# Moving loads to GpSimd's queue, listing first weight chunks one stage earlier, and reordering the end of the last block

## The chip, the cores and the metric

The kernel runs on one core of one Trainium2 chip. The metric is the device time of one execution in microseconds (us). An execution's time is a little longer than its span, which runs from the first to the last instruction of the program.

## What is computed

One residual block on 512 tokens of width 2048, in f32. A normalised input goes through one wide projection; its columns feed three branches and their gates. Each branch has its own output projection, the three are merged by sigmoid gates, and one last projection is added to the residual stream.

```python
h = rms_norm(x, norm_g)
proj = h @ w_in
(c_gate, b_gate, u, conv_z, c_q, c_kv, k_rope_raw, mla_z,
 mem_q, mem_z, g_conv, g_mla, g_mem) = jnp.split(proj, split_at, axis=-1)
conv_y = b_gate * causal_depthwise_conv(c_gate * u, conv_w)
o_conv = (conv_y * jax.nn.silu(conv_z)) @ w_conv_out
mla_y = mla_attention(c_q, c_kv, k_rope_raw, cos, sin, ...)        # 16 heads, chunk mask
o_mla = (mla_y * jax.nn.silu(mla_z)) @ w_mla_out
mem_y = memory_attention(mem_q, mem, ...)                          # 256 tokens, 4 heads
o_mem = (mem_y * jax.nn.silu(mem_z)) @ w_mem_out
merged = sigmoid(g_conv)*o_conv + sigmoid(g_mla)*o_mla + sigmoid(g_mem)*o_mem
x = x + merged @ w_o
```

## The kernel before

TensorE works in a reduced-precision f32 form, so every product is three matmuls: weights and activations are split into a high and a low part (`mm3`, lines 158 to 163). ScalarE rounds a weight chunk to its high part (`whi`), VectorE subtracts it from the raw chunk (`wlo`). The first two matmuls of a panel product need `whi` alone, the third needs `wlo`.

The stages follow each other: key/value projection of the memory tokens (line 510), the wide input projection `w_h` in 64 blocks (line 778), attention with the convolution branch's output projection mixed in (lines 1044 to 1088), memory attention (line 1153), the rest of the convolution's projection (line 1176), the attention's output projection `w_mla_out` in 8 blocks (line 1207), the memory branch's output projection (line 1244), and the last projection `w_o` in 8 blocks (line 1246). Stages named with "blocks" use `panels`: a block is 256 output features, four weight chunks of 512 KB, and per chunk 14 products of 256 columns, which is 42 matmuls. Each raw chunk also needs three sums on VectorE (`pair_weights`, lines 263 to 265) before it is split (268, 269). The first two blocks run their chunks in the order 0,1,2 / 0,1,2 / 3,3, so the last two of the eight activation pairs `xp` are wanted only with the seventh chunk.

Weight chunks are jobs in one Python list, `queue`. `take(ahead)` starts the jobs of the next chunks (load and sums) and converts those up to `ahead` in front. Jobs listed after a stage can't be started in it. The raw tile has three buffers, `whi` and `wlo` two each.

The order on SyncE (SP, the engine that issues the loads) and on TensorE is the order of the Python program; both queues are in order. The order on VectorE, ScalarE and GpSimd comes from a planner that simulates the program; on the chip these queues are in order too.

`gate_blocks` (line 1008) loads the sigmoid gates of the convolution branch; from group 1 on its tile `sb` has two buffers. `mem_pair` (line 1224) merges two output blocks of the memory branch: it loads gate and running sum into one tile `mg` with one buffer (1225, 1226), multiplies and adds (1228, 1229), builds the pair's sums and splits them (ScalarE line 249, VectorE line 250) into the activations of `w_o`. `make_mla` (1194) loads a gate block in each block of `w_mla_out`, and in block 6 six tiles of the memory branch. `finish` (735) stores sigmoid gates through ScalarE's queue (774). `panel_steps` (274) runs a block and adds its four PSUM banks up afterwards (301 to 307); `finish_o` (1271) adds the residual and stores.

## Time and profile before

| | us |
|---|---|
| three runs | 2202.24, 2200.24, 2202.16 (median 2202.16) |
| the profiled execution | 2199.24 |
| its span | 2197.4 |
| TensorE busy | 2132.2 (97%) |
| VectorE busy | 1744.8 (79%) |
| ScalarE busy | 1004.2 (46%) |
| GpSimd busy | 110.8 (5%) |
| mean granted TensorE clock | 0.989 |

Busy time of TensorE hides slow stretches: a matmul at a lower granted clock is busy for longer. So the stretches are read by how many matmuls start in them, beside a stretch without any wait.

### The profile page before, as it was taken

What the parts mean: (1) busy time and instruction counts of PE and PEld (TensorE: products, weight loads), DVE (VectorE), ACT (ScalarE), POOL (GpSimd) and SP (SyncE); (2) the same over time, 40 slices, a digit from 0 to 9 for tenths busy, and PEclk for the clock granted to TensorE, in tenths of its full rate; (3) what the DMA queues carried; (4) which work ended last, traced back from release to release, by engine and by line L of the source; (5) the groups of instructions that cost most, each with busy time, mean ns of one, the idle gap of its engine ahead of it and who ended that gap; (6) DMA issues with size and microseconds to landing.
All of it is one profiled execution on the core that took longest, in us unless ns stands there. A gap on an engine that the chain in (4) does not pass through costs nothing.

```text
span 2197.4 us, 38848 instructions
## 1 busy us (share of the span) xinstructions
PE 2132.2 (97%) x16040; PEld 2043.9 (93%) x16040; DVE 1744.8 (79%) x2763; ACT 1004.2 (46%) x1219; POOL 110.8 (5%) x149
## 2 busy tenths in 40 slices
PE   9999999999999999999999999999999899996998
PEld 8789999999999999999999998888888699985998
DVE  6986888888888888889777875888877778657887
ACT  6743444444334444444444444877764433322332
POOL 0000000000000000000000001221211100000000
PEclk9999999999999999999999999999999999998999
DMA  8633433334334334343444446123266855644443
GB/s 328 237 101 135 154 135 126 128 128 134 120 125 135 116 125 136 126 138 133 132 132 147 133 133 225 68 87 113 92 238 226 330 146 168 199 163 172 150 158 116
DMA packets 92289, 334.31 MB, mean 152 GB/s; under 512 B 10768, under 2 KB 11024, under 8 KB 90064
## 3 DMA queue, kind: packets, MB, share of 16 engines
q1 hardware_dynamic: 75024, 268.05, 36.0%
q0 software_dynamic: 8160, 38.54, 5.1%
q10 hardware_dynamic: 8928, 25.25, 3.3%
q8 instruction: 125, 2.05, 0.4%
q14 instruction: 52, 0.43, 0.1%
HBM read 273.34 MB, written 58.46 MB: 151 GB/s over the span
## 4 chain that ended last, share of the span: by engine, by line
PE 84%; DVE 7%; DMA 5%; ACT 3%; issue 1%; POOL 0%; SPq 0%; DVEq 0%; POOLq 0%; ACTq 0%
PE acc L161 15%; PE acc L163 15%; PE acc L162 15%; PE aux L161 12%; PE aux L163 12%; PE aux L162 12%; DVE wlo L269 2%; DMA sb<-gdram 1%; DMA raw<-in_w_h 1%; PE aux L970 1%; DMA amdram<-my 1%; DVE raw L263 1%; PE aux L953 1%; DMA raw<-in_w_mla_out 0%; PE aux L954 0%
## 5 line engine op out<-in xcount | busy, mean ns | idle before, releaser
L268 ACT ACTIVATE whi<-raw 128x1792 fp32r<-128x1792 f32 x304 | 517.4, 1703 | 796.3 <-PE acc L162 363.1
L269 DVE TENSOR_TENSOR wlo<-raw,whi 128x1792 fp32r<-128x1792 f32 x304 | 614.6, 2022 | 205.4 <-ACT whi L268 205.0
L163 PE MATMUL aux<-xp,wlo 128*128 128x256 f32 (+1 forms) x1712 | 479.8, 280 | 4.8 <-DVE wlo L269 4.7
L161 PE MATMUL aux<-xp,whi 128*128 128x256 f32 (+1 forms) x1712 | 480.7, 281 | 0.1
L162 PE MATMUL aux<-xp,whi 128*128 128x256 f32 (+1 forms) x1712 | 479.4, 280 | 0.0
L163 PE MATMUL acc<-xp,wlo 128*128 128x256 f32 x1680 | 469.5, 279 | 3.4 <-DVE wlo L269 3.4
L161 PE MATMUL acc<-xp,whi 128*128 128x256 f32 x1680 | 470.1, 280 | 0.0
L162 PE MATMUL acc<-xp,whi 128*128 128x256 f32 x1680 | 469.1, 279 | 0.0
L163 PEld LDWEIGHTS aux<-xp,wlo 128*128 128x128 f32 (+1 forms) x1712 | 321.3, 188 | 5.7 <-DVE wlo L269 5.7
L161 PEld LDWEIGHTS aux<-xp,whi 128*128 128x128 f32 (+1 forms) x1712 | 321.1, 188 | 0.5 <-ACT whi L268 0.5
L162 PEld LDWEIGHTS aux<-xp,whi 128*128 128x128 f32 (+1 forms) x1712 | 320.4, 187 | 0.0
L163 PEld LDWEIGHTS acc<-xp,wlo 128*128 128x128 f32 x1680 | 315.4, 188 | 4.4 <-DVE wlo L269 4.4
L161 PEld LDWEIGHTS acc<-xp,whi 128*128 128x128 f32 x1680 | 315.3, 188 | 0.0
L162 PEld LDWEIGHTS acc<-xp,whi 128*128 128x128 f32 x1680 | 314.7, 187 | 0.0
L263 DVE TENSOR_TENSOR raw<-raw 128x512 f32<-128x512 f32 x304 | 208.4, 686 | 46.9 <-DMA raw<-in_w_h 32.4
L155 DVE TENSOR_TENSOR wlo<-raw,whi 128x1024 fp32r<-128x1024 f32 (+2 forms) x91 | 101.7, 1121 | 49.9 <-ACT whi L154 49.4
L154 ACT ACTIVATE whi<-raw 128x1024 fp32r<-128x1024 f32 (+2 forms) x91 | 89.0, 978 | 105.5 <-PE acc L162 37.2
L265 DVE TENSOR_TENSOR raw<-raw 128x256 f32<-128x256 f32 x304 | 128.3, 422 | 6.3
L264 DVE TENSOR_TENSOR raw<-raw 128x256 f32<-128x256 f32 x304 | 128.1, 422 | 5.8
L161 PE MATMUL acc<-whi,blk 128*128 128x384 f32 (+1 forms) x224 | 86.1, 384 | 3.6 <-ACT whi L154 3.6
L336 POOL TENSOR_TENSOR rs_r<-rs_t,mhalf 128x2 f32<-128x2 f32 (+2 forms) x71 | 69.4, 987 | 289.9 <-DVE rs_t L335 225.6
L162 PE MATMUL acc<-wlo,blk 128*128 128x384 f32 (+1 forms) x224 | 81.6, 364 | 0.3 <-DVE wlo L155 0.3
(348 smaller groups left out, 3892.8 us busy)
## 6 DMA issues: line engine op xcount, KB each, us to landing
raw<-in_w_h SPq DMA_DIRECT2D x240, 512.0 KB, 3.5
raw<-in_w_mla_out SPq DMA_DIRECT2D x32, 512.0 KB, 3.7
raw<-in_w_o SPq DMA_DIRECT2D x32, 512.0 KB, 3.7
raw<-in_w_mem_kv SPq DMA_DIRECT2D x31, 512.0 KB, 7.3
gdram<-e ACTq DMA_DIRECT2D x24, 512.0 KB, 2.8
raw<-in_w_ukv SPq DMA_DIRECT2D x16, 512.0 KB, 5.5
raw<-in_w_conv_out SPq DMA_DIRECT2D x16, 512.0 KB, 8.9
aadram<-z POOLq DMA_DIRECT2D x8, 896.0 KB, 4.0
```

What stands on the lines that cost most here:

```text
L154: act.activation(hi[:, cols], raw[:, cols], AF.Copy)
L155: vec.tensor_tensor(out=lo[:, cols], in0=raw[:, cols], in1=r32(hi[:, cols]), op=ALU.subtract)
L161: nc.tensor.matmul(o, lhsT=s[0], rhs=m[0], start=start, stop=False, skip_group_check=shared)
L162: nc.tensor.matmul(o, lhsT=s[0], rhs=m[1], start=False, stop=False, skip_group_check=shared)
L163: nc.tensor.matmul(o, lhsT=s[1], rhs=m[0], start=False, stop=stop, skip_group_check=shared)
L263: vec.tensor_tensor(out=f[:, 4:6], in0=f[:, 1:3], in1=f[:, 0:1].to_broadcast([P, 2, 256]), op=ALU.add)
L264: vec.tensor_tensor(out=f[:, 6], in0=f[:, 5], in1=f[:, 1], op=ALU.add)
L265: vec.tensor_tensor(out=f[:, 7], in0=f[:, 6], in1=f[:, 3], op=ALU.add)
L268: act.activation(hi, f[:, 1:8], AF.Copy)
L269: vec.tensor_tensor(out=lo, in0=f[:, 1:8], in1=r32(hi), op=ALU.subtract)
L336: pool.tensor_tensor(out=r, in0=t, in1=mhalf[:, :n], op=ALU.pow)
L953: nc.tensor.matmul(sb[:, :n], lhsT=qr[:, cols], rhs=krh[:, :n], start=False, stop=False)
```

## The change

- The panel work of `w_h` is listed ahead of the memory projection's loop, and that of `w_mla_out` and the memory output's chunks ahead of the last loop over the convolution's projection. The look-ahead of the memory projection becomes a function of the step (2 in steps 8 to 29, else 1).
- Gate loads of convolution groups 1 to 3, and gate and sum loads of `mem_pair`, go from SP's queue to GpSimd's. The last six gate stores go from ScalarE's queue to GpSimd's.
- The six memory tiles are loaded one in each of the blocks 1 to 6 of `w_mla_out`.
- The order of the memory attention's steps among the convolution's is changed (`ORDER_MEM`; a digit is a step of that head, "4w" four units of three matmuls of the convolution).
- In the last chunk of the last block of `w_o` the products are sorted, so that the four PSUM banks finish one after the other; `tail_o` adds them up and the residual, and stores the two halves on ScalarE's and SP's queues.

```diff
-ORDER_MEM = "0 0 1 1 5w 0 0 2 3w 1 1 3 3w 0 0 2 2 3w 1 1 3 3 3w 2 2 2w 3 3 w 2 2 3 3"
+ORDER_MEM = "0 0 4w 1 1 4w 0 0 2 2w 1 1 3 3w 0 0 2 2 w 1 1 3 3 2w 2 2 3w 3 3 w 2 2 3 3"
...
-            whi, wlo = take(ahead)
+            whi, wlo = take(ahead(c) if callable(ahead) else ahead)
...
-            for kk in range(2):
+            each = [(kk, pr) for kk in range(2) for pr in PRODUCTS]
+            if tail is not None and c == nch - 1:
+                each.sort(key=lambda e: PRODUCTS.index(e[1]))
+            for kk, (w, xi, bk, half) in each:
...
         vec.tensor_tensor(out=e[:, 1:6:4], in0=b[0], in1=e[:, 4:5].to_broadcast([P, 2, H]), op=ALU.add)
+        if tail is not None:
+            tail(b, e)
+            yield
+            return
...
+    work = panels(xp, a["w_h"], len(SEQUENCE), lambda n: make(n), lambda n, e: finish(n, e), "aux")
+    queue.insert(32 + 15, [lambda: rotary_weights(), None])
     parts_of_x = all_parts()
...
-                             ahead=2 if grp else 1):
+                             ahead=lambda c: 2 if 0 < 8 * grp + c - 7 < 23 else 1):
...
-            act.dma_start(gdram[GATES[kind, i]], two(e))
+            (act if n < 58 else nc.gpsimd).dma_start(gdram[GATES[kind, i]], two(e))
...
-    work = panels(xp, a["w_h"], len(SEQUENCE), make, finish, "aux")
-    queue.insert(next(at for at in range(len(queue)) if at == 15), [rotary_weights, None])
...
+                nc.sync.dma_start(t, gdram[n])
             else:
                 t = pg.tile([P, 2, S], F32, tag="sb", name="sb", bufs=2)
-            nc.sync.dma_start(t, gdram[n])
+                nc.gpsimd.dma_start(t, gdram[n])
...
     pairs = new_pairs()
+    work = panels(xp, a["w_mla_out"], 8, lambda n: make_mla(n), lambda n, e: finish_mla(n, e))
+    for grp in range(3):
+        upcoming(*plain_jobs([a["w_mem_out"][grp][c] for c in range(4)], 512))
+    for grp in range(2):
+        upcoming(*plain_jobs([a["w_mem_out2"][grp][c] for c in range(4)], 256))
     for n, _ in enumerate(conv):
...
-            if n == 6:
-                for k in range(6):
-                    memory_block(k, pam)
+            if n > 0 and n < 7:
+                memory_block(n - 1, pam)
...
-        nc.sync.dma_start(two(t, 4), gdram[16 + n])
-        nc.sync.dma_start(two(t), mgdram[n])
+        nc.gpsimd.dma_start(two(t, 4), gdram[16 + n])
+        nc.gpsimd.dma_start(two(t), mgdram[n])
...
+    def tail_o(b, e):
+
+        xr = xrs[7]
+        x4 = xr.rearrange("p f (h n) -> p (f h) n", h=2)
+        vec.tensor_tensor(out=x4[:, 1], in0=e[:, 1], in1=x4[:, 1], op=ALU.add)
+        vec.tensor_tensor(out=e[:, 6:8], in0=b[1], in1=e[:, 5:6].to_broadcast([P, 2, H]), op=ALU.add)
+        vec.tensor_tensor(out=x4[:, 0], in0=x4[:, 0], in1=e[:, 7], op=ALU.add)
+        vec.tensor_tensor(out=x4[:, 2:4], in0=x4[:, 2:4], in1=e[:, 6:7].to_broadcast([P, 2, H]), op=ALU.subtract)
+        vec.tensor_tensor(out=x4[:, 0], in0=b[2][:, 0], in1=x4[:, 0], op=ALU.add)
+        nc.scalar.dma_start(out[14 * P:15 * P], xr[:, 0])
+        vec.tensor_tensor(out=x4[:, 2], in0=x4[:, 2], in1=b[1][:, 1], op=ALU.subtract)
+        vec.tensor_tensor(out=x4[:, 3], in0=b[2][:, 1], in1=x4[:, 3], op=ALU.add)
+        nc.sync.dma_start(out[15 * P:16 * P], xr[:, 1])
```

## Rows read from the trace of the kernel before

**Rows 1.** The page, the span in 40 slices: busy tenths of TensorE.
```profile
PE   9999999999999999999999999999999899996998
```
**Rows 2.** Busy time by stretch: length, each engine busy (instructions), granted clock, DMA share, GB/s.
```profile
400.00:420.00 20.00, 20.00 (x172) 20.00 (x172) 17.79 (x25) 7.42 (x6) 0.00 (x0) 1.00 0.36 111
...
107.00:157.00 50.00, 43.07 (x337) 41.43 (x336) 43.02 (x52) 21.45 (x18) 0.10 (x1) 0.97 0.34 110
...
1746.00:1760.00 14.00, 5.15 (x24) 4.75 (x24) 12.16 (x16) 3.29 (x2) 2.16 (x4) 0.63 0.66 237
1900.00:1908.00 8.00, 3.53 (x19) 3.04 (x18) 7.21 (x10) 3.28 (x2) 0.00 (x0) 0.69 0.52 89
2010.00:2042.00 32.00, 13.06 (x89) 12.11 (x87) 24.07 (x34) 10.31 (x7) 0.00 (x0) 0.73 0.46 164
```
**Rows 3.** Waits of TensorE: who waited for whom, us in total, times, longest.
```profile
PE acc L161 <- ACT whi L268: 23.5, 2, 16.0
...
PE aux L343 <- DVE p L1130: 3.0, 1, 3.0
```
**Rows 4.** Timeline of ScalarE, start of w_h: start, us, instruction, idle before and releaser.
```profile
111.49 1.70 ACT L268 ACTIVATE whi<-raw 128x1792 fp32r<-128x1792 f32 x1 [2.81 <-DVE raw L265]
```
**Rows 5.** The page, costliest groups: count, busy us, mean ns of one, idle before.
```profile
L263 DVE TENSOR_TENSOR raw<-raw 128x512 f32<-128x512 f32 x304 | 208.4, 686 | 46.9 <-DMA raw<-in_w_h 32.4
...
L264 DVE TENSOR_TENSOR raw<-raw 128x256 f32<-128x256 f32 x304 | 128.1, 422 | 5.8
```
**Rows 6.** The page, DMA issues: queue, count, KB each, median us to landing.
```profile
gdram<-e ACTq DMA_DIRECT2D x24, 512.0 KB, 2.8
...
acdram<-e POOLq DMA_DIRECT2D x8, 512.0 KB, 3.5
...
mq<-mqdram POOLq DMA_DIRECT2D x4, 1024.0 KB, 10.6
...
mg<-gdram SPq DMA_DIRECT2D x8, 512.0 KB, 3.4
```
**Rows 7.** Timeline of SP's queue at the start of attention.
```profile
1343.36 0.32 SPq L914 DMA_DIRECT2D krl<-krdram  x1
```
**Rows 8.** Timeline of GpSimd: issue of a load.
```profile
1631.82 0.54 POOL L1075 DMA_DIRECT2D mq<-mqdram  x1 [2.40 <-PE aux L343]
```
**Rows 9.** Timeline of VectorE in the memory attention.
```profile
1663.21 1.28 DVE L1118 TENSOR_REDUCE mx<-aux 128x2 f32<-128x512 f32 x2
```
**Rows 10.** Timeline of SP's queue at the start of w_mla_out.
```profile
1738.86 4.06 SPq L1018 DMA_DIRECT2D sb<-gdram  x2
1743.03 1.32 SPq L262 DMA_DIRECT2D raw<-in_w_mla_out  x3
```
**Rows 11.** Timeline of SP's queue in block 6 of w_mla_out.
```profile
1881.33 2.89 SPq L1187 DMA_DIRECT2D am<-amdram  x6
```
**Rows 12.** Timeline of SP's queue at the start of w_o.
```profile
2014.29 0.32 SPq L1225 DMA_DIRECT2D mg<-gdram  x1
...
2015.13 1.40 SPq L262 DMA_DIRECT2D raw<-in_w_o  x3
```
**Rows 13.** Timeline of ScalarE: splits of the first two chunks of w_o.
```profile
2024.92 3.27 ACT L268 ACTIVATE whi<-raw 128x1792 fp32r<-128x1792 f32 x2
```
**Rows 14.** Timeline of VectorE: first product of pairs 0 and 7, split of pair 7.
```profile
1942.06 1.37 DVE L1228 TENSOR_TENSOR mg<-acc,mg 128x512 f32<-128x512 f32 x2 [1.31 <-PE acc L163]
...
2031.29 1.28 DVE L1228 TENSOR_TENSOR mg<-aux,mg 128x512 f32<-128x512 f32 x2
...
2042.11 2.02 DVE L250 TENSOR_TENSOR xo<-mg,xo 128x1792 fp32r<-128x1792 f32 x1
```
**Rows 15.** Timeline of TensorE: the seventh chunk of w_o.
```profile
2061.91 0.28 PE L161 MATMUL acc<-xo,whi 128*128 128x256 f32 x1
```
**Rows 16.** Timeline of VectorE at the end.
```profile
2191.31 0.69 DVE L303 TENSOR_TENSOR e<-aux,e 128x512 f32<-128x512 f32 x1
...
2193.04 1.28 DVE L1274 TENSOR_TENSOR xr<-e,xr 128x512 f32<-128x512 f32 x2
```

More of the change, by code (lines that the diff above doesn't have):

```diff
@@ L272, in body, with panel_steps @@
     later, between = [], []
-    def panel_steps(xp, e, tag, middle=None):
+    def panel_steps(xp, e, tag, middle=None, tail=None):
         d = bank(tag)
@@ L290, in panel_steps @@
                 first, last = c == 0 and kk == 0, c == nch - 1 and kk == 1
-                for w, xi, bk, half in PRODUCTS:
-                    mm3(b[bk][:, half * H:(half + 1) * H], (whi[:, w, cols], wlo[:, w, cols]),
-                        (x[:, 0, xi], x[:, 1, xi]), first and half == 0, last, bk != 3)
+                mm3(b[bk][:, half * H:(half + 1) * H], (whi[:, w, cols], wlo[:, w, cols]),
+                    (x[:, 0, xi], x[:, 1, xi]), first and half == 0, last, bk != 3)
             if c == 2:
@@ L308, in panel_steps, with panels @@
         yield
-    def panels(xp, weight, n, make, finish, first="acc"):
+    def panels(xp, weight, n, make, finish, first="acc", tail=None):
         order = [(0, c) for c in range(3)] + [(1, c) for c in range(3)] + [(0, 3), (1, 3)]
@@ L323, in go @@
                     es[i], middle = make(i)
-                    steps[i] = panel_steps(xp, es[i], tags[i % 2], middle)
+                    steps[i] = panel_steps(xp, es[i], tags[i % 2], middle, tail if i == n - 1 else None)
                 next(steps[i])
-                if c == 3:
+                if c == 3 and (i < n - 1 or tail is None):
                     finish(i, es[i])
@@ L1205, in finish_mla @@
         nc.gpsimd.dma_start(mgdram[n], sgs[n], accum_op=ALU.add)
-    work = panels(xp, a["w_mla_out"], 8, make_mla, finish_mla)
-    for grp in range(3):
-        upcoming(*plain_jobs([a["w_mem_out"][grp][c] for c in range(4)], 512))
-    for grp in range(2):
-        upcoming(*plain_jobs([a["w_mem_out2"][grp][c] for c in range(4)], 256))
     for _ in work:
@@ L1245, in body @@
         if done == 7:
-            work = panels(xp, a["w_o"], 8, lambda n: make_o(n), lambda n, e: finish_o(n, e))
+            work = panels(xp, a["w_o"], 8, lambda n: make_o(n), lambda n, e: finish_o(n, e),
+                          tail=lambda b, e: tail_o(b, e))
         banks = [bank(tag) for _ in range(width // P)]
```

## The prediction

> **What bounds the kernel now.** The page comes first. TensorE is busy nearly all the time, and the 40 slices show where it is not: a dip after the memory attention and two towards the end [rows 1]. Next come stretches, read by how many matmuls start in them. The reader is to see 172 starts in 20.00 us in a quiet stretch: 0.1163 us per matmul of 256 columns, 4.88 us per chunk of 42, 19.5 us per block [rows 2]. What is missing from that count is lost, waits and slow matmuls alike. The waits of TensorE then name the kind: first chunks of a stage come late, as `whi` from ScalarE (L268), and once the memory attention's `p` [rows 3]. The timelines say what those engines waited for.
>
> Lost now, by the count: the start of `w_h`, 107 to 157, has 337 of 430 starts; 93 are missing, 10.8 us. The start of `w_mla_out`, 1746 to 1760, has 24 of 120.4: 11.2 us. Block 6 of it, 1900 to 1908, has 19 of 68.8: 5.8 us. The start of `w_o`, 2010 to 2042, has 89 of 275.2: 21.6 us [rows 2]. In the last three the mean granted clock is 0.63 to 0.73: with the wait, part of the time is granted the lower level (1.2 GHz), and the matmuls then are slow. The count has this in it.
>
> **The change, part by part** (minus is gained).
>
> *Start of `w_h`: -2.5.* ScalarE sat idle for 2.81 us before it could split the second chunk, until that chunk's sums were done [rows 4]; the sums are 0.69 + 2 x 0.42 = 1.5 us of VectorE [rows 5]. Listed earlier, these sums and the first chunk's split can run beside the memory projection. The first chunk's parts still need a buffer that the projection's last step but one releases, so part of the first wait stays. And VectorE is busy for 43.02 of the 50 us [rows 2] and loses no work. So I take the 1.5 us of sums and 1 us of the first wait. Bounds: 0 if VectorE's load decides everything, -6 if a good half of the 10.8 goes.
>
> *Last six gate stores: +0.6.* On GpSimd's queue a 512 KB store lands 3.5 us after its issue, on ScalarE's 2.8 [rows 6]. The attention's loads stood in SP's queue behind the landing of the last of these stores, until 1343.36 [rows 7], and a weight chunk that TensorE soon waits for is queued behind them. So up to 0.7 us more, nearly all on the path. Bounds 0 and +1.5 (with an issue of 0.54 us on GpSimd [rows 8]). ScalarE gets six issues back where nobody waits for it.
>
> *Memory attention's order: -1.5.* TensorE waited 3.0 us for head 0's `p` [rows 3]. Between head 0's scores and its transposes stand now eight units of the convolution instead of five, 3 x 0.67 us = 2.0 us more cover (a unit is six times 0.1163 us). But head 0's maximum was taken only at 1663.21 [rows 9], after splits of keys on VectorE that wait until head 1's scores are through, and these scores now come later; heads 1 and 2 get one and two units less. Between +1 and -3.5.
>
> *Start of `w_mla_out`: -8.* Two gate loads in SP's queue took from 1738.86 to the end of the row's 4.06 us, since the second stood there until a buffer came free, and the first three chunks of `w_mla_out` went out behind it at 1743.03 [rows 10]. From 1746 TensorE had nothing to do for 23.5 - 16.0 = 7.5 us [rows 2, 3]. Now the gates are out of SP's queue, and the first chunk's load stands in front of the last two loads of activation pairs. Its sums and split (1.5, 1.7 and 2.0 us [rows 4, 5, 14]) compete on VectorE with the last splits of the pairs, 2.0 us each. I leave one such split and 1 us of slow matmuls, 3 of the 11.2 us. Next late is VectorE, busy 12.16 of these 14 us [rows 2]. In GpSimd's queue the gate loads stand among stores of the memory attention and of the gated sums; what waits for them is the group's own product with the gates, and the banks that this frees are wanted only a block later. Bounds -3 and -11.
>
> *Memory tiles spread: -5.8.* Six loads of 512 KB were issued in 2.89 us [rows 11], in front of three weight chunks, and the loss of 5.8 us follows. Spread, a block's transfers become six or seven in 19.5 us; three raw buffers cover that. Bounds -4.5 and -6.
>
> *Start of `w_o`: -13.* SP stood before the loads of pair 6 until 2014.29, since `mg` has one buffer, and the first chunks of `w_o` went out at 2015.13 behind them [rows 12]. ScalarE split them from 2024.92 on [rows 13]; TensorE had waited 16.0 us by then [rows 3], so since about 2010.6 (2024.92 + 1.7 - 16.0). With the pairs in GpSimd's queue SP can load the first chunks while the memory output runs, and their sums and the first split lie beside it. What is late next is the pairs themselves: one buffer, so one pair after the other. Pair 0 began at 1942.06, pair 7 at 2031.29, 12.75 us each, and pair 7 was split by 2042.11 + 2.02 = 2044.1 [rows 14]. That didn't matter, since the seventh chunk, the first that reads it, ran at 2061.91 [rows 15]. Without the wait it could start at 2010.6 + 6 x 4.88 = 2039.9, so the pairs now decide. In GpSimd's queue a pair's two loads take longer: 0.54 us per issue [rows 8], and a landing up to 0.7 us later, going by the stores [rows 6]; I take 0.6 us for each of 8 pairs, 4.8. The seventh chunk then starts at 2048.9, 13.0 us earlier than before. Bounds: 0.2 us a pair, -16.2; 1.0 us a pair and 4 us of splits in each other's way, -6.
> A rule of the Trainium skill speaks against this part: "DMA: Bandwidth & Descriptors", section "Issuing engines are not separate DMA queues", says that starting transfers from several engines saves only the time of the issue. By it the move would be worth next to nothing. The row shows something the sentence doesn't count: the load at 2015.13 was not held by a transfer, it stood behind an instruction that waited for a buffer [rows 12].
>
> *End by product: -0.7.* Before, bank 1 was complete 6 matmuls (0.7 us) before the end, and its sum began at 2191.31; the residual's additions ended at 2193.04 + 1.28 = 2194.3 [rows 16]. With the products sorted bank 1 is complete 12 matmuls before the end, so at 2190.6. Behind it VectorE has two operations of 0.69 us [rows 16] and four of 0.42 us [rows 5], 3.1 us, so it ends at 2193.6 with a little overlap. Bounds -0.4 and -1.5.
>
> **Sum.** -2.5 + 0.6 - 1.5 - 8 - 5.8 - 13 - 0.7 = -30.9. Against the profiled execution's own time of 2199.24 that is 2168.3; the median of the runs, 2202.16, stands 2.9 us above that execution, so 2171 for the runs.
>
> **The rivals.**
> (a) *The planner keeps the chunks' splits behind the pairs' splits* on ScalarE and VectorE. For it: the first two chunks of `w_o` were split only at 2024.92, back to back [rows 13], with pair 6 in front. Against it: their loads had left at 2015.13 only [rows 12]. If so, the second chunk starts at 2026.6, the seventh at about 2055 (five chunks, one split of 2.0 us and 2 us of slow matmuls later), 7 us gained at `w_o` instead of 13, and a us less at `w_mla_out`: 2178.
> (b) *VectorE bounds both early listings.* For it: 43.02 of 50 and 12.16 of 14 us busy [rows 2]. Against it: the idle ScalarE in between [rows 4]. Nothing at `w_h`, 3 instead of 8 at `w_mla_out`: 7.5 us less, 2178.
> (c) *The change doesn't do what it says*: leaving SP's queue saves only issues. Then `w_mla_out` and `w_o` gain nothing, and -9.9 stays: 2192. The rule above would give this.
> (d) *Slower: GpSimd's loads are as slow as in the memory stage.* There a load in its queue took 10.6 us to land, SP's loads for the pairs 3.4 [rows 6]. The place is the chain of pairs. The other parts gain 17.9 us, so it decides once the seventh chunk starts later than 2061.91 + 17.9 = 2079.8: 4.5 us per pair over the old 2044.1. With all 7.2 us a pair it starts at 2101.7, 39.8 us late, 21.9 us slower on the whole: 2224. Against it: those loads are twice as large, GpSimd's 512 KB stores land in 3.5 us [rows 6], and the DMA share around the pairs is 0.46 [rows 2].
> The Trainium skill has a reason for such lateness ("SBUF — State Buffer", section "SBUF: two separate sides"): GpSimd's cores write the descriptors of these transfers and are locked out while VectorE runs a two-port operation, such as a plain f32 copy. The pairs use sums, differences and products of two tensors, not such copies, and the issue shown took 0.54 us [rows 8]; no run here shows it.
> (e) *Every part at its good end*: -44.2, 2158.
>
> **How the numbers follow.** The forecast as summed 0.50, (a) 0.18, (b) 0.13, (e) 0.08, (c) 0.05, (d) 0.04, and 0.02 for parts that cancel. All bad ends together give -11.4, 2191. The range 2158 to 2186 holds the forecast with nearly all its bounds, (a), (b) and half of (e): 0.83. Faster by over 0.2% (4.4 us, about what a measurement of this kernel can tell from no change) are all but (d) and the last: 0.94; the same 0.02; slower 0.04.
>
> **What would show it.** Right: some 8 us or less missing by the count at the start of `w_o`, its first chunk loaded before 2005, and the seventh chunk waiting for the last split of a pair, not for `whi`; the first load of `w_mla_out` well before the old stage ends; no dip in block 6; GpSimd's loads for the pairs landing in 4 to 5 us. Wrong: the first split of `w_o` still behind a pair's split, pair loads above 8 us, or matmuls lost in the long `w_h` stage, which I take as unchanged.

## The result, and the profile after

The changed kernel takes 2187.69 us (median of four runs, 2185.54 to 2191.75), the kernel before 2202.2 beside it (2200.24 to 2205.12, four runs). The ratio is 0.9935, with an interval of 0.9917 to 0.9953: faster by 0.65%, 14.5 us between the medians. The forecast was 2171, its range 2158 to 2186. The sign came as forecast, the gain was half of it, and the time lies above the range. The profiled execution of the kernel after takes 2187.3 us, its span is 2185.5, against 2197.4 before: 11.9 us to account for.

Cut at five points that both traces show (the end of `w_h`, the first scores of the memory attention, the first matmul of the memory output, the start of the twelfth chunk of `w_o`, the last matmul), the two spans compare so:

| stretch | before, us | after, us | difference | forecast for it |
|---|---|---|---|---|
| start to the end of `w_h` | 1336.4 | 1335.8 | -0.6 | -2.5 |
| to the memory attention's first scores | 320.1 | 313.1 | -7.0 | +0.6 |
| to the memory output's first matmul | 265.6 | 258.9 | -6.7 | -15.3 |
| to the twelfth chunk of `w_o` | 165.6 | 171.0 | +5.4 | -13.0 |
| to the last matmul | 103.9 | 102.0 | -1.9 | 0 |
| to the end | 5.9 | 4.8 | -1.1 | -0.7 |

Only the end came as summed. One stretch gives 7 us that I had not forecast, one gives less than half, and the largest term of the forecast has the wrong sign.

Each column is one execution. How far a stretch moves by itself is seen in the kernels of the experiments whose program is the same there. The second takes 313.0 to 314.4 us in the eleven that are like the kernel after. The third takes 253.5 to 257.1 us in seven, so the 258.9 in the table lie at its long end. The fourth takes 172.1 to 172.7 us in four, and 164.8 to 165.6 in the kernel before and three like it.

The page of the kernel after, the span in 40 slices, TensorE and its granted clock. Against [rows 1] the dip after the memory attention is gone; towards the end an 8 and a 7 stand where a 6 stood:

```profile
PE   9989999999999999999999999999999999998799
...
PEclk9999999999999999999999999999999999999899
```

Busy time by stretch, kernel after, columns as in [rows 2]:

```profile
107.00:157.00 50.00, 42.34 (x336) 41.28 (x337) 41.81 (x49) 21.57 (x18) 0.00 (x0) 0.97 0.32 107
1740.00:1754.00 14.00, 11.01 (x87) 10.19 (x85) 13.93 (x19) 5.50 (x4) 2.18 (x4) 1.00 0.51 167
1890.00:1898.00 8.00, 7.82 (x66) 7.62 (x66) 7.39 (x10) 1.70 (x1) 0.85 (x1) 1.00 0.49 165
1998.00:2046.00 48.00, 27.34 (x194) 26.61 (x193) 34.35 (x44) 13.49 (x8) 2.09 (x4) 0.79 0.41 146
```

By the count of matmul starts the start of `w_h` loses as much as before (336 against 337). At the start of `w_mla_out` 33 of 120 are missing instead of 96, while VectorE is busy for 13.93 of 14 us. Block 6 has lost its dip (66 of 68.8). At the start of `w_o` 219 of 413 are missing in 48 us, at a mean granted clock of 0.79: behind the waits, part of the time is again granted the lower level, 1.2 GHz.

The waits of TensorE, kernel after, with what answers to [rows 3]:

```profile
PE aux L161 <- DVE mg L1236: 15.0, 2, 14.4
...
PE acc L161 <- DVE mg L1236: 5.7, 1, 5.7
PE aux L163 <- DVE wlo L155: 4.7, 3, 2.8
```

The 23.5 us for `whi` are gone but for 0.6, and the 3.0 for `p` have become 1.5. In their place stand 20.7 us for L1236, and that is no operand of a matmul of `w_o`: it is the product of a pair of the memory output with its gate (L1228 before), the operation that reads a bank of the memory output and so frees it.

### The profile page after: what moved, and what is told of

It reads as the page before. It is cut to its first block, busy times and chain, and to the rows that moved or that the text cites. A ratio compares the mean times of both kernels' runs of the same rounds, so it can differ in the third digit from the quotient of the medians.

```text
span 2185.5 us, 38852 instructions
## 1 busy us (share of the span) xinstructions
PE 2128.3 (97%) x16040; PEld 2038.7 (93%) x16040; DVE 1741.5 (80%) x2764; ACT 1003.8 (46%) x1219; POOL 123.9 (6%) x173
## 4 chain that ended last, share of the span: by engine, by line
PE 81%; DVE 8%; DMA 4%; issue 4%; ACT 2%; POOL 0%; SPq 0%; DVEq 0%; POOLq 0%; ACTq 0%
PE acc L161 14%; PE acc L162 14%; PE acc L163 14%; PE aux L163 11%; PE aux L162 11%; PE aux L161 11%; DVE wlo L269 3%; DMA raw<-in_w_mla_out 1%; DMA raw<-in_w_o 1%; DVE raw L263 1%; PE aux L978 1%; DMA sb<-gdram 1%; DMA raw<-in_w_h 1%; PE aux L961 1%; DVE wlo L155 0%
## 5 line engine op out<-in xcount | busy, mean ns | idle before, releaser
L155 DVE TENSOR_TENSOR wlo<-raw,whi 128x1024 fp32r<-128x1024 f32 (+2 forms) x91 | 101.5, 1119 | 47.7 <-ACT whi L154 47.7
L161 PE MATMUL acc<-whi,blk 128*128 128x384 f32 (+1 forms) x224 | 84.8, 379 | 0.0
L163 PE MATMUL acc<-whi,blk 128*128 128x384 f32 (+1 forms) x224 | 80.9, 361 | 0.0
```

The source lines that it names most:

```text
L155: vec.tensor_tensor(out=lo[:, cols], in0=raw[:, cols], in1=r32(hi[:, cols]), op=ALU.subtract)
L161: nc.tensor.matmul(o, lhsT=s[0], rhs=m[0], start=start, stop=False, skip_group_check=shared)
L163: nc.tensor.matmul(o, lhsT=s[1], rhs=m[0], start=False, stop=stop, skip_group_check=shared)
```

## What the traces say of each place

**Start of `w_o`.** VectorE, ScalarE and GpSimd, kernel after (start, us, instruction, idle before and releaser), one line of each kind in the order of time:

```profile
1995.70 2.03 DVE L269 TENSOR_TENSOR wlo<-raw,whi 128x1792 fp32r<-128x1792 f32 x1
2000.81 0.69 DVE L263 TENSOR_TENSOR raw<-raw 128x512 f32<-128x512 f32 x1 [3.08 <-DMA raw<-in_w_o]
...
2002.34 2.02 DVE L269 TENSOR_TENSOR wlo<-raw,whi 128x1792 fp32r<-128x1792 f32 x1
2004.27 1.28 DVE L1236 TENSOR_TENSOR mg<-acc,mg 128x512 f32<-128x512 f32 x2
...
2020.16 1.28 DVE L1236 TENSOR_TENSOR mg<-aux,mg 128x512 f32<-128x512 f32 x2
...
2036.12 1.29 DVE L1236 TENSOR_TENSOR mg<-aux,mg 128x512 f32<-128x512 f32 x2 [4.12 <-DMA mg<-gdram]
```
```profile
2010.47 1.70 ACT L268 ACTIVATE whi<-raw 128x1792 fp32r<-128x1792 f32 x1 [10.67 <-PE acc L162]
2012.08 1.68 ACT L249 ACTIVATE xo<-mg 128x1792 fp32r<-128x1792 f32 x1
```
```profile
1995.36 0.53 POOL L1233 DMA_DIRECT2D mg<-gdram  x1 [14.58 <-DVE xo L250]
```

TensorE at the two long waits, with the wait in brackets:

```profile
2005.01 0.58 PE L161 MATMUL acc<-xo,whi 128*128 128x256 f32 x1 [5.66 <-DVE mg L1236]
...
2036.87 0.58 PE L161 MATMUL aux<-xo,whi 128*128 128x256 f32 x1 [14.40 <-DVE mg L1236]
```

GpSimd issues pair 5's loads at 1995.36, when pair 4's last split has freed the buffer. While they are under way, VectorE takes up `w_o`'s chunks, which SP had loaded early, as meant. It then stands for 3.08 us before the sums of a chunk whose load has not landed, does these and a split, and comes to pair 5's product at 2004.27. TensorE has wanted that bank since 1999.3. ScalarE stands for 10.67 us before the third chunk's split, since TensorE holds its buffer, with pair 5's split (L249) behind it. So one queue's wait becomes the other's. The longest wait, 14.40 us, comes in the same way: pair 6's sums stand between those of the chunks on VectorE, its split there ends at 2032.0, only then does GpSimd issue pair 7's loads (2032.30), and VectorE stands 4.12 us until they land. The products of pairs 4 to 7 start at 1983.56, 2004.27, 2020.16 and 2036.12: 20.7, 15.9 and 16.0 us apart, where 12.3, 11.8 and 13.7 lay between them before.

**The loads on GpSimd.** DMA issues, kernel after, as in [rows 6] (queue, count, KB, median us to landing):

```profile
mg<-gdram POOLq DMA_DIRECT2D x8, 512.0 KB, 3.7
mg<-mgdram POOLq DMA_DIRECT2D x8, 512.0 KB, 4.7
sb<-gdram POOLq DMA_DIRECT2D x6, 512.0 KB, 7.6
gdram<-e POOLq DMA_DIRECT2D x2, 512.0 KB, 4.0
```

The pairs' gate loads land in 3.7 us, 3.4 before, and are issued in 0.53 us, 0.54 in [rows 8]; the convolution's land in 7.6, 6.9 before. Rival (d), slow loads for the pairs, is out.

**Start of attention.** SP's queue, kernel after; in [rows 7] the second of these stood until 1343.36:

```profile
1331.25 0.42 SPq L922 DMA_DIRECT2D krl<-krdram  x1
...
1332.74 0.83 SPq L196 DMA_DIRECT2D raw<-in_w_uq  x2
```

What had held it is in the waits of SP's queue, kernel before, 1325 to 1350:

```profile
SPq L914 <- DMA gdram<-e: 11.5, 1, 11.5
```

A load of the rotary key had waited for the landing of a gate store that it has nothing to do with. The semaphores in the trace's records say why. At this place each transfer that SP or ScalarE issues reports to one of eight completion counters (semaphores 100, 102 and 105 to 110), taken in turn by both, and SP first waits until the transfer before it on the same counter has reported. In the kernel before, ScalarE's last gate store and `krl` have the same one; the store's last part reports at 1343.34, and `krl` is issued at 1343.36. GpSimd's transfers have other counters, 113 and 114 for the two stores that were moved. Time of issue and semaphores, kernel before:

```
1338.84  ScalarE  L774  gdram<-e      reports to 100
1343.36  SP       L914  krl<-krdram   waits for 100, reports to 100
1343.72  SP       L915  tabs<-csdram  waits for 102, reports to 102
```

**Start of `w_mla_out`.** VectorE, kernel after:

```profile
1714.38 1.29 DVE L1040 TENSOR_TENSOR sb<-acc,sb 128x512 f32<-128x512 f32 x2 [3.88 <-DMA sb<-gdram]
...
1746.70 1.28 DVE L1040 TENSOR_TENSOR sb<-aux,sb 128x512 f32<-128x512 f32 x2
...
1752.43 3.95 DVE L269 TENSOR_TENSOR wlo<-raw,whi 128x1792 fp32r<-128x1792 f32 x2
```

At 1714 VectorE stands 3.88 us before the product with a gate; the gate's load, now in GpSimd's queue, was issued at 1702.26 behind a store that itself waited for VectorE. A weight split stands behind the product, and TensorE waits 2.8 us for it, where 0.5 stood before. From 1731 on VectorE works without a gap: the last activation pairs, the chunks' sums, the gate products, and the split of the third and fourth chunk only at 1752.43.

By place: from the memory attention's first scores to the first matmul of `w_mla_out` the kernel after takes 91.0 us, 97.1 before; from there to the memory output 167.9, 168.6 before, although the spread tiles alone take 4.1 off this second part (below).

## The experiments

"The way" below is the time from the first matmul of the memory output to the start of `w_o`'s twelfth chunk: 165.6 us before, 171.0 after.

**One part alone: the gate stores.**

```diff
-            act.dma_start(gdram[GATES[kind, i]], two(e))
+            (act if n < 58 else nc.gpsimd).dma_start(gdram[GATES[kind, i]], two(e))
```

> The kernel before with one edit: the gate stores from block 58 on (the last two) go out in GpSimd's queue. In the built program each transfer that SP or ScalarE issues takes one of eight completion counters in turn, and the load of krl waits for the counter that the last gate store of ScalarE had. Theory: only this counter held SP until 1343.36. So SP issues krl at about 1331.5 and the first load of w_uq at about 1333 (before 1344.74), the loss of 7 us at the attention's start is gone, and the time is 2195, within 2193 to 2197 (2202 before). Rival: the gain at the attention's start came from the earlier listing of w_h's chunks or another part; then the time moves by less than 1.5 us and SP still stands until about 1343.

Measured: SP issued `krl` at 1333.87 and `w_uq` at 1335.36, and the 20 us after the end of `w_h` held 96 matmul starts, where the kernel before has 66 (rows below, the first of the experiment, then before). The stretch to the memory attention's first scores takes 314.3 us: 5.8 of the 7.0 that the whole change gained there, and within the spread of the kernels like the kernel after. The time was 2197.23 (ten runs; 0.2 above what was expected), ratio 0.9964 with an interval of 0.9949 to 0.9978, 7 us between the medians. This edit by itself gives the attention's gain, within that spread.

```profile
1338.00:1358.00 20.00, 19.24 (x96) 16.73 (x95) 9.35 (x20) 10.95 (x27) 4.58 (x5) 1.00 0.73 273
```
```profile
1336.00:1356.00 20.00, 16.09 (x66) 13.45 (x65) 8.23 (x19) 9.42 (x24) 3.41 (x4) 0.85 0.61 225
```

SP's wait for the store is not gone, though: it now stands behind the first loads of `w_uq`, and between 1330 and 1375 TensorE waits for no weights longer than 0.6 us (waits of SP's queue, 1325 to 1352; 9.0 us in the kernel after). Why the load of a latent block waits for that store no run here separates.

```profile
SPq L822 <- DMA gdram<-e: 9.5, 1, 9.5
```

**The held load taken out of SP's queue instead.**

```diff
-    nc.sync.dma_start(r32(krl), krdram[:, 1])
+    nc.gpsimd.dma_start(r32(krl), krdram[:, 1])
```

> The kernel before with one edit: the load of krl itself goes out in GpSimd's queue, the gate stores stay with ScalarE. Theory (shared counter): the counter of the last gate store now falls to the next load of SP, tabs; it stands until about 1343.4 instead, the first load of w_uq goes out at 1344 to 1345 as before, and the loss at the attention's start stays near 7 us. Rival (krl waited for its own data or buffer): SP is free, w_uq goes out at 1332 to 1334, and the loss of 7 us is gone.

Measured, the waits of SP's queue in this kernel:

```profile
SPq L915 <- DMA gdram<-e: 12.2, 1, 12.2
```

The counter fell to the next load, `tabs` (L915), as the theory of the shared counter had it: in this trace `tabs` waits for semaphore 100. `w_uq` went out at 1347.47, 8.5 us after `w_h`'s end (8.3 before), and that place was 6.7 us longer than in the kernel after, 7.0 before. It was never `krl`'s own data.

**One part undone: the pairs' loads back in SP's queue.**

```diff
-        nc.gpsimd.dma_start(two(t, 4), gdram[16 + n])
-        nc.gpsimd.dma_start(two(t), mgdram[n])
+        nc.sync.dma_start(two(t, 4), gdram[16 + n])
+        nc.sync.dma_start(two(t), mgdram[n])
```

> The kernel after with one edit undone: the loads of the memory output's pairs are back in SP's queue. Theory (in GpSimd's queue they let the w_o chunks' sums and splits stand ahead of the pairs' products on VectorE and ScalarE, and these products free TensorE's banks too late): the bank waits for L1236, 20 us in the kernel after, fall below 6 us, the wait of 16 us for whi comes back, the way from the start of the memory output to the twelfth chunk of w_o falls from 171.0 to 165 to 167 us, and the time is 2183, within 2180 to 2186 (2188 after). Rival: the 5 us lost there come from the memory tiles or from what the earlier stages shifted; then the way stays at 169 to 172 us and the time at 2186 to 2190.

Measured: 2184.78, ratio 0.9909 (0.9885 to 0.9933); the way is 165.2 us, as before. The wait for `whi` is back, the bank waits are gone (waits of TensorE, 1900 to 2070):

```profile
PE acc L161 <- ACT whi L268: 16.4, 1, 16.4
```

So on the way this part of the change cost 5.8 us. It changed one wait for another, longer one. Between the runs' times the difference to the kernel after (2.9 us) is no more than their spread; the way in the trace carries the statement, and it is clear of the spread of the way in kernels that are alike there (171.0 to 172.7 in five, 164.8 to 165.6 in four).

**The pairs' loads left out.**

```diff
-        nc.gpsimd.dma_start(two(t, 4), gdram[16 + n])
-        nc.gpsimd.dma_start(two(t), mgdram[n])
         for i in range(2):
-            vec.tensor_tensor(out=two(t, 4)[:, i], in0=banks[i], in1=two(t, 4)[:, i], op=ALU.mult)
+            vec.tensor_tensor(out=two(t, 4)[:, i], in0=banks[i], in1=late_blocks[0][:, i]..., op=ALU.mult)
...
```

> The kernel after with the pairs' two loads left out: the memory gates and the sums gathered so far are not loaded, the product uses a memory tile in their place and is added to itself. Theory A (one buffer: each pair's 4 to 5 us of loading lies on the chain of pairs): the distances between the products of pairs 4, 5, 6 and 7, 20.7, 15.9 and 16.0 us, shrink by about 4 us each, the bank waits of 20 us fall to 6 to 12 us. Theory B (the chunks' work ahead of them on VectorE alone sets the distances): they stay within 2 us of what they were, and the bank waits above 16 us.

Measured: the way fell to 147.4 us, and no bank wait is left. The products of pairs 4 to 7 came 9.3, 12.1 and 16.2 us apart. That is more than theory A asked for between pairs 4 and 5, and nothing between 6 and 7. So the loads are the larger part of it, through more than their own 5 us: without them a pair's work on VectorE comes in one piece, and the chunks' work doesn't slip in ahead. This run alone can't tell the buffer from the order.

**The order on VectorE and ScalarE written out.**

```diff
+        if done == 6:
+            listed.enter_context(tc.manual_schedule(engines={DVE, mybir.EngineType.Activation}))
...
+        if at == 4:
+            listed.close()
```

> The kernel after; from the last group but one of the memory output to the fifth chunk of w_o the operations of VectorE and ScalarE stand in the order in which the kernel lists them, so pairs 5 and 6 come ahead of the sums and splits of w_o's first chunks. Loads, buffers and queues are as in the kernel after. Theory (the order in the two engines' queues spaced the pairs' products): the distances between the products of pairs 4, 5, 6 and 7 fall from 20.7, 15.9 and 16.0 us to 12 to 14 each, the wait for pair 5's bank (5.7 us) goes, that for pair 7's (14.4 us) falls to 6 to 10, the way from the start of the memory output to the twelfth chunk of w_o falls from 171.0 to 157 to 163 us, and the time is 2178, within 2174 to 2183. Rival (GpSimd's loads and the single buffer spaced them): distances above 15 us, way 168 to 172, time 2186 to 2190.

Measured: 2188.52, ratio 0.9944 (0.9929 to 0.9959), the way 170.9 us, against 171.0. And yet part of the theory came: products 13.0, 12.1 and 17.6 us apart, where 12 to 14 each were expected, and no bank wait. The waits of TensorE, 1900 to 2070, show where the time went:

```profile
PE aux L163 <- DVE wlo L155: 8.8, 3, 6.7
PE aux L161 <- ACT whi L154: 6.3, 1, 6.3
```

Now the memory output's own chunks stand behind the pairs, which wait for their loads (VectorE idle 4.06 us before pair 4's product, 3.50 before pair 5's). The theory that the order did it fell here: with one buffer, the landing of a pair's loads is a hole in VectorE's queue, and whatever stands behind the pair waits through it, the banks or the chunks.

**Two buffers.** Pairs 5 and 7 take a raw weight tile, whose shape is the same, one of the three that the weight chunks use.

```diff
-        t = pm.tile([P, 8, H], F32, tag="mg", name="mg", bufs=1)
+        t = raw_tile() if n in (5, 7) else pm.tile([P, 8, H], F32, tag="mg", name="mg", bufs=1)
```

> The kernel after; pairs 5 and 7 of the memory output use a buffer of the weights' raw tiles instead of the one of mg, so that their loads don't wait for the pair in front. The order on VectorE and ScalarE is left to the planner. Theory (a pair's buffer is free only after its last split, so load and work of the pairs come one after the other, and the banks wait for that): the product of pair 5 follows that of pair 4 within 8 us (20.7 before), pair 7's follows pair 6's within 8 us (16.0), bank waits fall from 20 us to below 5, the way to the twelfth chunk of w_o falls from 171.0 to 150 to 157 us, time 2172, within 2167 to 2179. Rival (the chunks' work ahead of the pairs is what counts): distances stay above 12 us, way above 163.

Measured: 2174.97, ratio 0.9888 (0.9873 to 0.9903), the way 157.9 us. Pair 5's product now comes even before pair 4's (1971.90 and 1980.48), and pair 7's 11.5 us after pair 6's, farther than expected. No bank wait is left; the largest is

```profile
PE aux L163 <- DVE wlo L155: 6.1, 3, 2.7
```

Against the kernel before that is 0.5% more than the kernel after gained (0.9888 and 0.9935), for one buffer. So the single buffer is what made the early loads of `w_o` a loss; the way came out a little above the 150 to 157 us that I expected, and the largest wait left is for splits of VectorE. One thing stays unseparated: a pair in a raw tile takes this tile from the weight chunks, and `w_o`'s first matmul comes 96 us after the memory output's here, 90 in the kernel after. A second buffer of `mg` itself was not tried.

**Both.**

> Both edits of the two runs in front: two buffers for the pairs and the listed order on VectorE and ScalarE. If the order and the buffer both hold the banks, the way is shorter than with either alone, 148 to 154 us, and the time 2170, within 2165 to 2176. If two buffers already take all of it, the way is as with them alone, within 2 us.

Measured: 2182.04, ratio 0.9922 (0.9906 to 0.9939), the way 163.4 us, worse than two buffers alone. Neither sentence of the expectation holds: the written order costs 5.5 us of the way against the planner's, which lets chunks pass.

**The convolution's gates listed earlier.**

```diff
+                if at == 12 and pg is not None:
+                    gates_of[grp] = gate_blocks(grp)
```

> The kernel after; the gate loads of a group of the convolution are listed 12 units into its group instead of at its end, about 13 us earlier in GpSimd's queue. Theory (VectorE stood 3.9 us at the product with a gate that landed late, and the weight split behind it came 2.95 us late for TensorE): that wait at 1714 goes, 1700 to 1720 loses below 1.5 us instead of 4.2, and the time is 2184.5, within 2182 to 2187. Rival (the transfers there are late because the DMA engines are full, 12 to 18 us per load): the gate lands late all the same or other weights come later for it; loss of 3 us or more, time 2186 to 2190.

Measured: 2188.97, ratio 0.995 (0.9935 to 0.9964): no gain in the time. VectorE still stood 2.73 us before the gate product. TensorE's wait for the split behind it is 1.6 us instead of 2.8, and the way from the memory attention's scores to `w_mla_out` 88.3 us instead of 91.0; but six kernels without this edit have 1.7 or 1.8 us and 88.3 to 88.8 us as well, so it is the kernel after whose execution stands out here, and nothing is shown for the edit. In the last stretch this kernel ran at the slower of two paces (last section), 3.7 us more than the kernel after.

**Less work for VectorE at the start of `w_h`.**

```diff
-        vec.tensor_tensor(out=f, in0=f, in1=xscale.unsqueeze(1).to_broadcast([P, 2, S]), op=ALU.mult)
```

> The kernel after with the multiplication by the rows' scale left out of the eight activation pairs of w_h: one operation of VectorE of 1.22 us per pair, and nothing else. Theory (VectorE bounds the start of w_h, so that sums listed earlier only stand in front of the last pair's sums): with this work gone the window from 107 to 157, 336 matmul starts in both kernels so far, holds 355 or more. Rival (the buffers that the memory projection releases, or the loads, bound it): it holds 334 to 345.

**The listing of `w_h` undone**, and with it the look-ahead of the memory projection.

```diff
-    work = panels(xp, a["w_h"], ..., "aux")     # ahead of the memory projection
+    work = panels(xp, a["w_h"], ..., "aux")     # behind it, as before
```

> The kernel after with one part undone: the chunks of w_h are listed after the memory projection again, as in the kernel before, and the look-ahead there is the old one. Theory (the earlier listing gave nothing): the window of 50 us from the end of the projection holds 336 matmul starts, within 3, and w_h ends within 1.5 us of the kernel after, 1335.8, counted from the end of the projection. Rival (it gave the 2.5 us that the prediction summed, and something else took them back): w_h ends 2 to 3 us later.

Measured, busy time by stretch, first without the multiplication, then with the listing undone (its projection ends 2 us later, so its window is moved by 1):

```profile
107.00:157.00 50.00, 46.57 (x374) 45.59 (x373) 40.91 (x51) 24.55 (x23) 0.10 (x1) 0.97 0.39 130
```
```profile
108.00:158.00 50.00, 44.33 (x336) 42.84 (x335) 41.99 (x49) 21.89 (x18) 0.10 (x1) 0.93 0.33 111
```

The first shows that this work bounds the window: 374 starts instead of 336. It doesn't tell VectorE's load from the chain of the last activation pairs, since the operation left out stands in both. The second holds 336, as the kernel after does: the listing gave nothing that this window can show. From the end of the projection `w_h` took 1230.5 us with it undone, 1229.0 in the kernel after, 1228.9 before; but in ten kernels that don't differ there it took between 1227.6 and 1233.6, and the window held 311 to 349 starts in four of them. So 0 is the best reading, 2 us can't be excluded, and 374 is outside that spread. The one run with the listing undone took 2193.46, above all four of the kernel after; one run decides nothing.

**Memory tiles alone**, on the kernel before.

```diff
-            if n == 6:
-                for k in range(6):
-                    memory_block(k, pam)
+            if n > 0 and n < 7:
+                memory_block(n - 1, pam)
```

> The kernel before with one part of the change: a memory tile is loaded in each of blocks 1 to 6 of w_mla_out instead of six in block 6. Theory (the six loads in a row held the next weight chunks, and nothing else changes): the dip in block 6, 6.5 us in the kernel before, goes, and the way from the first chunk of w_mla_out to the memory output falls from 168.6 to 162 to 163 us. Rival (the spread loads come in the way of the other blocks' chunks, which would explain the small waits of 3.6 us in the kernel after): small waits of 2 us or more stand in blocks 1 to 7, and the way is 165 us or more.

Measured: the place of the dip holds 66 starts in 8 us, 19 before [rows 2]; the way from the first chunk to the memory output is 164.5 us, 4.1 less. By the spacing of the matmuls 1.6 us are lost in small pieces in later blocks instead. It lies between the two expectations: the dip of 6.5 us went, and about a third came back.

```profile
1899.00:1907.00 8.00, 7.82 (x66) 7.61 (x65) 7.49 (x10) 1.70 (x1) 0.85 (x1) 1.00 0.52 180
```

**The listing of `w_mla_out` undone.** In the kernel after, its chunks are listed behind the convolution again.

```diff
-    work = panels(xp, a["w_mla_out"], ...)      # ahead of the convolution's last group
+    work = panels(xp, a["w_mla_out"], ...)      # behind it, as before
```

> The kernel after with one part undone: the chunks of w_mla_out are listed after the convolution again; the gate loads stay in GpSimd's queue and the memory tiles spread. Theory (at the start of w_mla_out VectorE has the last splits of the activation pairs, the gate products and the chunks' sums and splits to do, so that listing the chunks earlier moves the wait and takes little away): the way from the memory attention's start to the memory output, 258.9 us in the kernel after, comes out within 3 us of that. Rival (the earlier listing gave the 5.4 us by which the loss between 1740 and 1760 fell, and without it they are back): 263 us or more.

Measured: from the memory attention's scores to the memory output 258.6 us, in the kernel after 258.9, as the theory had it. But seven other kernels with the earlier listing take 253.5 to 257.1 there, so it gave between 0 and 5 us, and some 3 is the best reading. Most of what it does is to move the loss: without it `w_mla_out` starts later (93.1 us after the scores, 88.3 to 91.0 with it), and takes 165.5 us from there (165.1 to 167.9 with it). Without it TensorE waits in one piece (waits, 1710 to 1760), with it in several. The one run took 2192.90.

```profile
PE acc L161 <- ACT whi L268: 4.9, 1, 4.9
```

**Combined versions.** The first has the two buffers and the earlier gates; in the second every odd pair takes the second buffer.

```diff
-        t = raw_tile() if n in (5, 7) else pm.tile(...)
+        t = raw_tile() if n % 2 else pm.tile(...)
```

> The kernel after with two edits that each helped their own stretch: two buffers for pairs 4 to 7 of the memory output, and the gate loads of the convolution listed 12 units into their group. If the two are independent, the way to w_o's twelfth chunk is 156 to 160 us and the way from the memory attention's start to the first chunk of w_mla_out 88 to 89 us, and the time is 2172, within 2168 to 2177 (2188 after). If the transfers get in each other's way it is 2177 or more.

> As the combined kernel, but every odd pair (1, 3, 5, 7) takes the second buffer, not 5 and 7 alone. Theory (the pairs' chain is bound by the buffer from the first pair on): pairs 3 and 4 come earlier too, another 2 to 4 us less on the way to the twelfth chunk, 153 to 156 us, time 2169. Rival (the raw buffers are then short for the memory output's own chunks, 4 of w_mem_out per buffer of two): the memory output waits for whi or wlo of its own, and the way is 158 us or more.

Measured: 2178.52 (0.9904, 0.9887 to 0.992) and 2174.66 (0.9877, 0.9857 to 0.9896). In the first the two stretches are as expected (88.6 and 158.8 us), but two buffers alone have 88.5 and 157.9, so the earlier gates add nothing, and the time lies 1.5 us above what was expected, where the rival was placed. With every odd pair the way is 156.8 us, between theory and rival; the rival's wait is there too (3.5 us for L155). Against two buffers alone neither is a gain that these runs can tell. Two buffers, for two pairs or for four, take less time than both kernels: their intervals (0.9873 to 0.9903 and 0.9857 to 0.9896) lie below that of the kernel after.

## Why the prediction was wrong, step by step

**Start of `w_o`, -13 forecast, +5.4 measured: the step that failed.** It has two faults. First, "the pairs now decide", through the seventh chunk that reads the last pair: I asked who reads what a pair writes, and not what a pair's product sets free. The first chunk of `w_o` goes into the banks of pairs 4 and 5, the fourth into those of 6 and 7. Before, this cost nothing, since the first chunk came at 2026.7 and the fourth at 2047.1, and the products of pairs 5 and 7 had begun at 2005.8 and 2031.3, the second in [rows 14]. With the wait for `whi` gone, the banks were next, three chunks ahead of my seventh. By an estimate from these rows this alone would have cut the gain to some 10 us (the fourth chunk from 2047.1 to 2031.3 + 1.3 + 4.8). Second, I kept the pairs' distance at 12.75 us and added 0.6 for the queue. What I should have added is what the change puts on VectorE in between: the chunks' sums and splits, with waits for loads of their own. The distances became 20.7, 15.9 and 16.0 us, and the gain turned into a loss. The part undone gives 5.8 us back; a second buffer, with the loads left in GpSimd's queue, gives 13.1. My rival (a) had the two in each other's way, but in the opposite order, chunks behind pairs. In the written-out order this came true, and it cost as much.

The signs that I had named: the first chunk's load did leave early (1980.67), and the seventh chunk did not wait for `whi`. Nor did it wait for a pair's split. I had allowed for 8 us missing at this place; the 219 matmuls missing in 48 us are 25.

**Start of `w_mla_out`, -8, and the order in the memory attention, -1.5.** Together with the tiles 15.3 us were summed and 6.7 came. The wait for `p` fell from 3.0 to 1.5 us, as summed. (Two slips in the prediction's count, without weight in its sum: heads 1 and 2 get two and three units less, not one and two, and a unit, six times 0.1163 us, is 0.70, not 0.67.) The tiles are 4.1 of their 5.8. That leaves about 1 us for the 8 in this execution, and 3 to 6.5 in the seven other kernels that are alike there, where rival (b), VectorE as the bound, had said 3. The window at the stage's start did lose 7 us less (33 matmuls missing instead of 96), but part of it came back: in the wait at 1714 ahead of it and in small waits of the blocks behind it. At 1740 to 1754 VectorE is busy for 13.93 of 14 us. And the gates, for which I had said that only a bank wanted a block later waits, held VectorE itself, an engine whose queue has weight splits in it: TensorE waited 2.8 us, 1.6 to 1.8 in most other kernels. That wait is measured; no run took it away.

**Start of `w_h`, -2.5.** Nothing came, as rival (b) had it. ScalarE, first two lines the kernel after, then before:

```profile
108.83 1.69 ACT L268 ACTIVATE whi<-raw 128x1792 fp32r<-128x1792 f32 x1
...
116.64 1.70 ACT L268 ACTIVATE whi<-raw 128x1792 fp32r<-128x1792 f32 x1 [3.68 <-PE aux L162]
```
```profile
116.85 1.70 ACT L268 ACTIVATE whi<-raw 128x1792 fp32r<-128x1792 f32 x1 [1.21 <-PE aux L163]
```

The idle 2.81 us of [rows 4] did go: the second chunk is split at 108.83 instead of 111.49. But the first chunk's first matmul came as late as before (107.84, 107.6 before), its split behind that of an activation pair, and the third chunk's split, which waits for a buffer that TensorE holds, at 116.64 instead of 116.85. The gain became a longer wait there. Idle time of ScalarE was no sign that TensorE would gain by it.

**Gate stores, +0.6 forecast, -7.0 measured.** I had the wait and its end right, read the landing of the store as a dependence on data, and so charged the longer landing of GpSimd's store (4.0 us). It was a counter in common, and another queue has other counters. This wrong step went in the kernel's favour: 7.0 of the 11.9 us that the spans differ by come from a part that I had put at a small loss. That the sign of the whole came out right owes much to this luck. Of the stores moved there are two, not six as the prediction says (`n` reaches 59; `w_h` has 60 blocks, not the 64 of the description).

**Memory tiles, -5.8:** right in mechanism, 4.1 in size where they were the only change. **End by product, -0.7:** right, 1.1; VectorE's last operation ended at 2182.5, 1.7 us behind the last matmul's start:

```profile
2182.06 0.41 DVE L1297 TENSOR_TENSOR xr<-aux,xr 128x256 f32<-128x256 f32 x1
```

**The rivals.** (c), that leaving a queue saves only the issue, drew on the Trainium skill, "DMA: Bandwidth & Descriptors", "Issuing engines are not separate DMA queues". The landing times agree with the rule (3.4 and 3.7 us for the same load in two queues), but the time doesn't follow from it: leaving the queue gave 7 us in one place and cost 5.8 in another. Neither is transfer time; both are what stands behind a waiting instruction. (d) is refuted by the 3.7 and 4.7 us in which the pairs' loads land. The range missed since its lower gains came from parts that fail one by one; I gave no case in which the largest part turns into a loss while the others shrink.

## What to carry to other kernels

When a wait is taken away, list all that the late engine needs at that point, the banks it writes as well as the tiles it reads, and when each is free. Work that is released early lands in somebody's in-order queue: look whose, and what stands behind it; here VectorE, busy for 13.93 of 14 us, had no room at one place, and at the other a buffer more was worth what a new order was not. And where a queue stands before a load that needs nothing, ask what else the instruction waits for: a completion counter that it shares with another engine's transfer can hold it. Before an edit is credited with 2 or 3 us of one trace, look at the same stretch in kernels that don't differ there; here it moved by 5.

## What the hardware showed that I had not expected

Shared completion counters, above: 7 us at one place, moved from one load to the next by taking the first out.

TensorE has two paces at the same granted clock. Busy time by stretch, 2100 to 2120, in three kernels (before, after, `krl` on GpSimd):

```profile
2100.00:2120.00 20.00, 20.00 (x172) 20.00 (x171) 17.03 (x23) 7.20 (x5) 0.00 (x0) 1.00 0.49 157
```
```profile
2100.00:2120.00 20.00, 20.00 (x178) 20.00 (x177) 17.27 (x25) 8.13 (x6) 0.00 (x0) 1.00 0.50 159
```
```profile
2100.00:2120.00 20.00, 20.00 (x177) 20.00 (x178) 17.69 (x25) 7.60 (x6) 0.00 (x0) 1.00 0.48 149
```

172 or 178 starts in 20 us, without a wait and at 1.00: 0.116 or 0.112 us per matmul of 256 columns. The quicker pace came and went within one execution, too: with the pairs back in SP's queue 179 at 2040 to 2060 and 172 at 2100 to 2120. It goes with no part of the change, and is worth up to 3.7 us in the last stretch. The 1.9 us of that stretch in the table are no more than this pace gives. What sets it no run here shows; it stays open.
